# Moving where tiles start in SBUF: split inputs and DeltaNet outputs at multiples of 2048 bytes in a hybrid attention layer

## The chip, the cores and the metric

The kernel runs on one core of a Trainium2 chip. The metric is device time in microseconds (us) of one execution, the median over several runs. TensorE (PE) multiplies matrices; its weights are loaded by a queue of their own (PEld). VectorE (DVE), ScalarE (ACT) and GpSimd (POOL) work on tiles in SBUF; SyncE (SP) issues the DMAs. SBUF has 128 partitions, and a tile takes the same range of bytes in each of them, so "where a tile starts" is one byte offset within a partition.

## The reference

One layer of a diffusion backbone on 512 latent tokens after 256 context tokens, width 1024. All arithmetic is float32.

```python
hx = modulate(rms_norm(x), sh1, sc1);  hc = modulate(rms_norm(ctx), csh1, csc1)
ak, av, qkv, db, da, aq, z, gate = split_cols(hx @ w_in)     # context: the first columns only
attn_x = latent_attention(q_x, [k_c, k_x], [v_c, v_x])       # 8 heads of 128, 2 kv heads
o_x    = gdn_bidirectional(gdn_c_in, gdn_x_in)               # gated DeltaNet, 8 heads, both directions
gdn_x  = rms_norm(o_x, norm_w) * silu(z)
y = sigmoid(g_a) * (attn_x @ w_pa) + sigmoid(g_d) * (gdn_x @ w_pd)
x = x + g1 * (y @ w_out)
x = x + g2 * conv_ffn(modulate(rms_norm(x), sh2, sc2), w_up, ffn_conv_w, ffn_conv_b, w_down)
return rms_norm(x, final_norm_w)
```

Within a chunk the DeltaNet solves a unit lower triangular system `(I + strict(beta * dec * k k^T))`; everything else in it is small matrix products.

## The kernel before, in words

Every large product is made of three matmuls. A float32 operand is split in two words of a shorter format, `hi` (ACT copies and rounds) and `lo` (DVE subtracts), and `mm3` adds `hi*xh`, `hi*xl` and `lo*xh` in PSUM. The weights `whi`/`wlo` are the stationary operand, 128 columns at a time; the activations are the moving operand, 512 latent or 256 context columns at a time, 8 steps over the width. So one step of a latent projection is three 128x512 matmuls that read 2048 bytes of each partition of `xH` or `xL`.

The split activations are `hxH`/`hxL` (the modulated input, latent) and `hcH`/`hcL` (context), `atH`/`atL` (attention output), the `g` tiles (DeltaNet output), `yH`/`yL`, `h2H`/`h2L` and `aH`/`aL`. `at`, `y`, `h2` and `a` are allocated with `align_bytes=2048`. `hx` lies in the pool `hxp`, the first one on the right end of SBUF; it is read by 48 latent projections (24 of queries, keys and values, 8 of `z`, 16 of gates) and, as the stationary operand, by the attention's query, key and value projections (`pq`), and with the narrow weights `dbh`/`dbl` (32 columns) by the decays. The `g` tiles have no room of their own: `gsplit` puts them into slots of DeltaNet tiles that are no longer needed, `q4` (names `g_s`), `NN` (`g_n`), `kT` (`g_k`) and `M2` (`g_m`).

Pools are stacks: `cp` (constants and small columns), `ws` (weights) and then the pools of each stage grow from the left end, `hxp`, `stp`, `hcp` and later `yp`, `fp` from the right end. A pool that opens later lies over the bytes of one that was closed, and with `reuse_waits="tile"` a tile there waits for the old tiles that it overlaps.

The order is written out by hand: TensorE's instructions keep the program's order (`pinned`). During attention (about 190 to 362 us) the projections are woven between heads. After it come four pairs of DeltaNet heads. For a pair, `gdn_prep` loads `kT` and the decay rows `NN`, `Gb`; `gdn_solve` inverts the 32x32 diagonal blocks in 31 steps of two operations (`prod`, `R`), on POOL for pairs 1 to 3 and on DVE for pair 0, with `X`, `R`, `C`, `o_tr`, `o_nt` in three slots of the tag `q4`; `gdn_inv` completes the inverse on TensorE; `gdn_scan` runs over the chunks. The solve of the next pair runs beside the inverse and the scan of this one, and `weave` puts filling work (`filler`: the remaining projections, then `w_pa`, then `w_pd`) between them at fixed rates. From about 880 us on `w_out`, `w_up` and `w_down` follow with nothing woven in.

```python
q4 = lambda nm: gq.tile([P, 32, 32], F32, name=nm, tag="q4", bufs=3)
...
for j in range(31):
    ...
    tt(pv, X[:, j, j + 1:32].unsqueeze(2).to_broadcast([P, m, n]),
       R[:, j:j + 1, 0:n].to_broadcast([P, m, n]), ALU.mult, eng)
    tt(R[:, j + 1:32, 0:n], R[:, j + 1:32, 0:n], pv, ALU.add, eng)
```

Of the kernel before, what the change touches and what calls it, by code (L numbers as in the profile page):

```python
# [6 lines left out]
F32 = mybir.dt.float32  # L7
F32R = mybir.dt.float32r
# [6 lines left out]
P = 128  # L15
# [4 lines left out]
NA = NL + NCX  # L20
# [4 lines left out]
NH = 8  # L25
# [47 lines left out]
C_ID, C_ONE, C_MS, C_MI, C_TRI = 0, 128, 256, 512, 768  # L73
# [5 lines left out]
def hybrid_layer_body(tc, x, ctxt, xT, consts, cols, rows, w_mod1, w_mod2, w_db, w_aq, w_cm, w_pa, w_pd, w_out,  # L79
# [21 lines left out]
    es = ExitStack()  # L101
# [5 lines left out]
    def tt(out, a, b, op, eng=None):  # L107
        (eng or V).tensor_tensor(out=out, in0=a, in1=b, op=op)  # L108
# [7 lines left out]
    def stt(out, a, s, b, op0, op1):  # L116
        V.scalar_tensor_tensor(out=out, in0=a, scalar=s, in1=b, op0=op0, op1=op1)  # L117

    def act(out, a, f=AF.Copy, **kw):
        A.activation(out, a, f, **kw)  # L120
# [10 lines left out]
    def mm(ps, a, b, start=True, stop=True):  # L131
        T.matmul(ps, a, b, start=start, stop=stop)

    with es:
        cp = es.enter_context(tc.tile_pool(name="cp", bufs=1))
# [9 lines left out]
        def sooner():  # L145
            return tc.high_priority(offset=3000000)

        def solver():
            return tc.high_priority(offset=SOLVE)
# [1 line left out]
        def early():  # L151
            return tc.high_priority(offset=1000000)

        cst = cp.tile([P, C_TRI], F32, name="cst")
        with sooner():
            SP.dma_start(cst[:, 0:C_MS], consts[:, 0:C_MS])
        ident = cst[:, C_ID:C_ID + 128]
# [7 lines left out]
            ts(col[:, S_BMOD + o:S_BMOD + o + 8], col[:, S_BMOD + o:S_BMOD + o + 8], 1.0, ALU.add)  # L165
        mhalf = cp.tile([P, 32], F32, name="mhalf")
        V.memset(mhalf, -0.5)
        mod = cp.tile([P, 48], F32, name="mod")
        modc = cp.tile([P, 16], F32, name="modc")
        csl = cp.tile([P, KT], F32, name="csl")  # L170

# [43 lines left out]
        szd = [dp.tile([P, NL], F32, name=f"szd{i}") for i in range(NH)]  # L215
        atd = [dp.tile([P, NL], F32, name=f"atd{i}") for i in range(NH)]

        beta = cp.tile([P, 96], F32, name="beta")
        gam = cp.tile([P, 96], F32, name="gam")
        ngam = cp.tile([P, 96], F32, name="ngam")  # L220
        eg = cp.tile([P, 96], F32, name="eg")
        kdec = cp.tile([P, 96], F32, name="kdec")
        hks = [cp.tile([P, 6], F32, name=f"hk{i}") for i in range(NH)]
        glast = cp.tile([P, 96], F32, name="glast")
        qsc = [cp.tile([P, 8], F32, name=f"qsc{i}") for i in range(4)]
        rkk = [cp.tile([P, 6], F32, name=f"rkk{i}") for i in range(NH)]
# [188 lines left out]
        with m1_es:  # L415
# [11 lines left out]
            for op in LORD.split():  # L427
                i = int(op[1])
                with sooner():
# [3 lines left out]
                    elif op[0] == "h":  # L433
                        h, part = order[i]
# [421 lines left out]
        gq = ge.enter_context(tc.tile_pool(name="gq", bufs=1, reuse_waits="tile"))  # L856
# [15 lines left out]
        rqh = lambda p, hh: rkq[2 * p + hh]  # L872

        def gdn_prep(p, eng=G):
            kT = gq.tile([P, 2, NA], F32, name="kT", tag="kT", bufs=2)
            for hh in range(2):
                SP.dma_start(kT[:, hh, :], kTd[2 * p + hh])
            g = gq.tile([P, 32], F32, name="g", tag="g", bufs=2)
            gT = gq.tile([P, 32], F32, name="gT", tag="gT", bufs=2)
            V.memset(g[:, 24:32], 0.0)  # L880
            for d in range(2):
                for hh in range(2):
                    r0 = d * 48 + (2 * p + hh) * 6
                    u = slice(12 * d + 6 * hh, 12 * d + 6 * hh + 6)
                    stt(g[:, u], beta[:, r0:r0 + 6], -1.0, rkk[2 * p + hh], ALU.mult, ALU.mult)
                    tt(g[:, u], g[:, u], rkk[2 * p + hh], ALU.mult)
            V.transpose(gT, g)
            NN = gq.tile([P, 12, P], F32, name="NN", tag="NN", bufs=2)
            for hh in range(2):
                u = slice(6 * hh, 6 * hh + 6)  # L890
                Gb = gq.tile([P, 6, P], F32, name="Gb", tag="Gb", bufs=1)
                for d, D in ((0, NN[:, u, :]), (1, Gb)):
                    r0 = d * 48 + p * 12 + hh * 6
                    SP.dma_start(D.rearrange("p a b -> p (a b)"),
                                 gamdr[r0:r0 + 6, :].rearrange("a b -> (a b)").partition_broadcast(P))
                    tt(D, D, msk_s[d].unsqueeze(1).to_broadcast([P, 6, P]), ALU.add, eng)
                    for c in range(6):
                        act(D[:, c, :], D[:, c, :], AF.Exp, scale=-1.0, bias=gam[:, r0 + c:r0 + c + 1])
                tt(NN[:, u, :], NN[:, u, :], Gb, ALU.add, eng)
            return [kT, gT, NN]  # L900

        def gdn_solve(pre, eng):
            kT, gT, NN = pre
            for hh in range(2):
                for (c0, n) in ((0, 4), (4, 2)):
                    pb = gks.tile([P, 4, P], F32, name="pk", tag="pk")
                    for i in range(n):
                        sl = slice((c0 + i) * P, (c0 + i + 1) * P)
                        mm(pb[:, i, :], kT[:, hh, sl], kT[:, hh, sl])
                    u = slice(hh * 6 + c0, hh * 6 + c0 + n)  # L910
                    with sooner():
                        tt(NN[:, u, :], NN[:, u, :], pb[:, 0:n, :], ALU.mult)
                    yield
            with solver():
                q4 = lambda nm: gq.tile([P, 32, 32], F32, name=nm, tag="q4", bufs=3)
                C = q4("C")
                for b in range(4):
                    sb = slice(32 * b, 32 * b + 32)
                    V.transpose(C[sb, :, 12:24].rearrange("p j u -> p u j"), NN[sb, :, sb])
                    act(C[sb, :, 0:12], NN[sb, :, sb].rearrange("p u j -> p j u"))  # L920
                G.memset(C[:, :, 24:32], 0.0)
                X = q4("X")
                V.transpose(flat(X), flat(C))
                tt(X, X, gT.unsqueeze(2).to_broadcast([P, 32, 32]), ALU.mult)
                R = q4("R")
                G.memset(R, 0.0)
                G.memset(flat(R)[:, 0:1024:33], 1.0)
                if True:
                    for j in range(31):
                        m, n = 31 - j, j + 1  # L930
                        prod = gq.tile([P, 272], F32, name="prod", tag="prod")
                        pv = prod[:, 0:m * n].rearrange("p (i k) -> p i k", k=n)
# [3 lines that stand above are left out]
                tt(R, R, gT.unsqueeze(2).to_broadcast([P, 32, 32]), ALU.mult)  # L936
                o_tr = q4("o_tr")
                V.transpose(o_tr.rearrange("p u s -> p s u"), R)
                o_nt = q4("o_nt")
                V.transpose(o_nt.rearrange("p u s -> p s u"), R.rearrange("p i k -> p k i"))  # L940
            pre += [o_tr, o_nt]
# [210 lines left out]
        def gsplit(h):  # L1152
            if h % 2 == 0:
                if h < 4:
                    ts_ = [gq.tile([P, 32, 32], F32R, name="g_s", tag="q4", bufs=3) for _ in range(2 if h == 0 else 1)]
                    if h == 2:
                        ts_.append(gq.tile([P, 12, P], F32R, name="g_n", tag="NN", bufs=2))
                elif h == 4:
                    ts_ = [gq.tile([P, 12, P], F32R, name="g_n", tag="NN", bufs=2),
                           gq.tile([P, 2, NA], F32R, name="g_k", tag="kT", bufs=2)]  # L1160
                else:
                    ts_ = [gq.tile([P, 2, NA], F32R, name="g_k", tag="kT", bufs=2)]
                    ls = [gpool[0].tile([P, 2, 2, P], F32R, name="g_m", tag="M2", bufs=4) for _ in range(2)]
                    ls = [l.rearrange("p a b c -> p (a b c)") for l in ls]
                ts_ = [flat(t) for t in ts_]
                for i in range(2):
                    lo = ts_[1][:, 512 * i:512 * i + 512] if h < 6 else ls[i]
                    gHL[h + i] = (ts_[0][:, 512 * i:512 * i + 512], lo)
            return gHL[h]
# [13 lines left out]
        with early():  # L1183
            pre = gdn_prep(0, V if P0 else G)
# [113 lines left out]
        pinned[0] = True  # L1298
        weave(wait(WK), 1.0)
        weave(gdn_solve(pre, G if 0 in SPOOL else V), RK)  # L1300
        weave(wait(W0), 1.0)
        def stage(p, pre, nxt):
# [6 lines left out]
        for p in range(NP):  # L1309
            cur = pre  # L1310
            pre = gdn_prep(p + 1) if p + 1 < NP else None
            g = stage(p, cur, pre)
            weave(g, RI if p else RI0)
            while not gpool or len(ready) < 2 * p + 2:
                next(fill)
            g = gdn_scan(p, cur, gdn_load(p))
            out = (None, gdn_out(0), gdn_out(1), gdn_reload())[p]
            weave(both(g, out) if p > 0 else g, RS)
            weave(wait(W1), 1.0)
# [264 lines left out]
```

## Time and profile before

| | |
|---|---|
| median of 3 runs | 1305.97 us (1303.61 to 1308.03) |
| the profiled execution | 1306.96 us |
| its span, first to last instruction | 1304.3 us |
| mean granted TensorE clock | 0.978 |
| busy: PE, PEld, DVE, ACT, POOL | 94%, 79%, 65%, 48%, 24% |

The span is what the trace covers; 2.7 us of the execution lie around it. Matmuls are pipelined: the duration in a row runs until the result is out, and the next matmul starts before that, so the spacing of two starts tells the rate and the duration doesn't. The chain that ended last is followed back from the last instruction, at each step to what released it.

### The profile page before, as it was taken

The numbers are of one execution on the slowest core, as the hardware profiler recorded it, in microseconds if no ns is written. First come the engines' busy times: TensorE is split into PE (matmuls) and PEld (weight loads), VectorE is DVE, ScalarE is ACT, GpSimd is POOL, SyncE is SP. The second block draws the span as 40 slices with busy tenths as digits, with TensorE's granted clock in tenths as the row PEclk, the third lists the DMA queues.
The fourth block names the chain that finished last, engine by engine and source line by source line (L and its number), as shares of the span: only waits on it lengthen the run. The fifth ranks groups of instructions, "written<-read, shape, count | busy, mean of one in ns | idle before, by whom it ended". The sixth has DMA issues, their size and how long they took to land.

```text
span 1304.3 us, 20850 instructions
## 1 busy us (share of the span) xinstructions
PE 1229.6 (94%) x7835; PEld 1031.3 (79%) x7835; DVE 848.4 (65%) x1625; ACT 626.3 (48%) x1403; POOL 308.3 (24%) x364
## 2 busy tenths in 40 slices
PE   7899999999968999899998999999999999999997
PEld 4487878999857877778787878788988888888886
DVE  5886987777759986685665556555576666663323
ACT  5453656666576665474453443233354444443221
POOL 1752420000143249559447300000000000000000
PEclk8999999999998999899999999999999999999998
DMA  8656631121373342543533555265043222233331
GB/s 321 227 169 197 223 118 62 65 86 50 111 252 105 124 140 91 177 131 110 178 120 116 170 165 168 92 219 190 9 129 97 97 97 95 91 94 97 90 100 65
DMA packets 70789, 170.80 MB, mean 131 GB/s; under 512 B 7872, under 2 KB 18720, under 8 KB 69280
## 3 DMA queue, kind: packets, MB, share of 16 engines
q1 hardware_dynamic: 70688, 169.47, 39.4%
q8 instruction: 61, 1.00, 0.3%
q14 instruction: 40, 0.33, 0.1%
HBM read 144.23 MB, written 25.21 MB: 130 GB/s over the span
## 4 chain that ended last, share of the span: by engine, by line
PE 66%; POOL 10%; DVE 9%; DMA 5%; ACT 4%; issue 3%; SPq 0%; POOLq 0%; DVEq 0%; ACTq 0%
PE mc L87 32%; PE mb L87 17%; PE pq L87 4%; POOL R L108 4%; POOL prod L108 4%; PE pb L87 3%; PE pS L87 3%; PE ab L87 2%; PE ab L91 1%; DMA Gb<-gamdr 1%; PE xb L91 1%; DVE wlo L108 1%; PE pk L87 1%; DMA sz<-gdr 1%; POOL NN L108 1%
## 5 line engine op out<-in xcount | busy, mean ns | idle before, releaser
L108 DVE TENSOR_TENSOR wlo<-wraw,whi 128x1024 fp32r<-128x1024 f32 x152 | 187.6, 1235 | 162.6 <-ACT whi L120 161.6
L120 ACT ACTIVATE whi<-wraw 128x1024 fp32r<-128x1024 f32 x152 | 159.1, 1048 | 205.5 <-PE mc L87 106.5
L87 PE MATMUL mb<-hxH,whi 128*128 128x512 f32 x384 | 165.1, 430 | 2.1 <-DVE R L108 1.9
L87 PE MATMUL mb<-hxL,whi 128*128 128x512 f32 x384 | 155.0, 404 | 0.0
L87 PE MATMUL mb<-hxH,wlo 128*128 128x512 f32 x384 | 154.3, 402 | 0.0
L87 PE MATMUL mc<-h2L,whi 128*128 128x512 f32 (+1 forms) x376 | 142.7, 379 | 0.0
L87 PE MATMUL mc<-h2H,whi 128*128 128x512 f32 (+1 forms) x376 | 142.3, 378 | 0.3 <-ACT whi L120 0.3
L87 PE MATMUL mc<-h2H,wlo 128*128 128x512 f32 (+1 forms) x376 | 140.8, 374 | 0.5 <-DVE wlo L108 0.5
L108 POOL TENSOR_TENSOR rc<-rc,mhalf 128x2 f32<-128x2 f32 x4 | 3.3, 818 | 459.4 <-DVE rc L114 459.4
L87 PEld LDWEIGHTS mb<-hxH,wlo 128*128 128x128 f32 x384 | 74.0, 193 | 18.3
L87 PEld LDWEIGHTS mb<-hxH,whi 128*128 128x128 f32 x384 | 74.6, 194 | 13.9 <-ACT t L120 2.1
L87 PEld LDWEIGHTS mb<-hxL,whi 128*128 128x128 f32 x384 | 74.6, 194 | 10.3
L87 PEld LDWEIGHTS mc<-h2H,whi 128*128 128x128 f32 x376 | 70.6, 188 | 14.9 <-ACT whi L120 0.5
L87 PEld LDWEIGHTS mc<-h2H,wlo 128*128 128x128 f32 x376 | 70.6, 188 | 14.7 <-DVE wlo L108 1.0
L87 PEld LDWEIGHTS mc<-h2L,whi 128*128 128x128 f32 x376 | 70.7, 188 | 12.2
L87 PE MATMUL mc<-aH,whi 128*128 128x512 f32 (+1 forms) x198 | 72.9, 368 | 0.6 <-DVE x L117 0.6
L87 PE MATMUL mc<-aL,whi 128*128 128x512 f32 (+1 forms) x198 | 73.0, 369 | 0.0
L87 PE MATMUL mc<-aH,wlo 128*128 128x512 f32 (+1 forms) x198 | 72.0, 364 | 0.0
L117 DVE SCALAR_TENSOR_TENSOR u<-mc,col,u 128x511 f32<-128x511 f32 x88 | 65.3, 746 | 1.4
L108 POOL TENSOR_TENSOR prod<-X,R 128x31 f32<-128x31 f32 (+15 forms) x93 | 53.5, 576 | 22.3 <-DVE X L108 15.4
L108 POOL TENSOR_TENSOR R<-R,prod 128x31 f32<-128x31 f32 (+15 forms) x93 | 57.1, 613 | 6.8
L87 PE MATMUL pq<-whi,hxH 128*128 128x256 f32 x192 | 56.6, 295 | 0.0
(354 smaller groups left out, 3078.3 us busy)
## 6 DMA issues: line engine op xcount, KB each, us to landing
wraw<-in_w_cm_dram SPq DMA_DIRECT2D x48, 512.0 KB, 3.9
wraw<-in_w_up_dram SPq DMA_DIRECT2D x44, 512.0 KB, 3.7
wmd<-in_w_mod_dram SPq DMA_DIRECT2D x64, 256.0 KB, 3.8
wm<-in_w_mod_dram SPq DMA_DIRECT2D x8, 1024.0 KB, 8.2
wraw<-in_w_down_dram SPq DMA_DIRECT2D x16, 512.0 KB, 3.5
wraw<-in_w_aq_dram SPq DMA_DIRECT2D x12, 512.0 KB, 4.8
M<-gamdr SPq DMA_DIRECT2D x64, 64.0 KB, 4.4
wraw<-in_w_pa_dram SPq DMA_DIRECT2D x8, 512.0 KB, 4.0
```

Of the source, the lines that this page charges most:

```text
L87: i = nc.tensor.matmul(*a, **k)
L91: i = nc.tensor.transpose(*a, **k)
L108: (eng or V).tensor_tensor(out=out, in0=a, in1=b, op=op)
L117: V.scalar_tensor_tensor(out=out, in0=a, scalar=s, in1=b, op0=op0, op1=op1)
L120: A.activation(out, a, f, **kw)
```

## The change

A new pool `cr` on the right end, opened ahead of `hxp` and never closed, takes `cst`, `mod`, `beta`, `gam` and the first of the eight `hk` columns out of `cp`. The tags `kT`, `NN` and `q4`, and the `g` tiles that share their slots, are allocated with `align_bytes=2048`. No operation is added or removed.

```diff
+        cr = es.enter_context(tc.tile_pool(name="cr", bufs=1, side="right"))
-        cst = cp.tile([P, C_TRI], F32, name="cst")
+        cst = cr.tile([P, C_TRI], F32, name="cst")
...
-        mod = cp.tile([P, 48], F32, name="mod")
+        mod = cr.tile([P, 48], F32, name="mod")
...
-        beta = cp.tile([P, 96], F32, name="beta")
-        gam = cp.tile([P, 96], F32, name="gam")
+        beta = cr.tile([P, 96], F32, name="beta")
+        gam = cr.tile([P, 96], F32, name="gam")
...
-        hks = [cp.tile([P, 6], F32, name=f"hk{i}") for i in range(NH)]
+        hks = [(cp if i else cr).tile([P, 6], F32, name=f"hk{i}") for i in range(NH)]
...
-            kT = gq.tile([P, 2, NA], F32, name="kT", tag="kT", bufs=2)
+            kT = gq.tile([P, 2, NA], F32, name="kT", align_bytes=2048, tag="kT", bufs=2)
...
-            NN = gq.tile([P, 12, P], F32, name="NN", tag="NN", bufs=2)
+            NN = gq.tile([P, 12, P], F32, name="NN", align_bytes=2048, tag="NN", bufs=2)
...
-                q4 = lambda nm: gq.tile([P, 32, 32], F32, name=nm, tag="q4", bufs=3)
+                q4 = lambda nm: gq.tile([P, 32, 32], F32, name=nm, align_bytes=2048, tag="q4", bufs=3)
...
-                    ts_ = [gq.tile([P, 32, 32], F32R, name="g_s", tag="q4", bufs=3) for _ in range(2 if h == 0 else 1)]
+                    ts_ = [gq.tile([P, 32, 32], F32R, name="g_s", align_bytes=2048, tag="q4", bufs=3) for _ in range(2 if h == 0 else 1)]
```

The other tiles of `gsplit` (`g_n` twice, `g_k` twice) get the same argument; `g_m` does not.

## Rows read from the trace of the kernel before

**Rows 1.** The page: TensorE's busy time, share and instructions; the chain by engine.

```profile
PE 1229.6 (94%) x7835; PEld 1031.3 (79%) x7835; DVE 848.4 (65%) x1625; ACT 626.3 (48%) x1403; POOL 308.3 (24%) x364
...
PE 66%; POOL 10%; DVE 9%; DMA 5%; ACT 4%; issue 3%; SPq 0%; POOLq 0%; DVEq 0%; ACTq 0%
```

**Rows 2.** The chain in order of time, end of a solve: start us, us, what.

```profile
531.01 0.26 POOL R L108
...
533.18 1.83 DVE o_tr L938
...
537.08 2.08 PE pb L87 x8
```

**Rows 3.** TensorE in order of time: first and last matmul of five unbroken sequences.

```profile
100.31 0.39 PE L87 MATMUL mb<-hxH,dbh 128*32 128x512 f32 x1
...
105.59 0.39 PE L87 MATMUL mb<-hxH,dbl 128*32 128x512 f32 x1
...
748.34 0.40 PE L87 MATMUL mb<-hxL,whi 128*128 128x512 f32 x1
...
752.77 0.40 PE L87 MATMUL mb<-hxH,wlo 128*128 128x512 f32 x1
...
809.57 0.39 PE L87 MATMUL mb<-atL,whi 128*128 128x512 f32 x1
...
811.18 0.40 PE L87 MATMUL mb<-atH,wlo 128*128 128x512 f32 x1
...
848.01 0.40 PE L87 MATMUL mb<-g_s,wlo 128*128 128x512 f32 x1
...
853.60 0.39 PE L87 MATMUL mb<-g_s,wlo 128*128 128x512 f32 x1
...
1099.76 0.39 PE L87 MATMUL mc<-h2H,whi 128*128 128x512 f32 x1
...
1105.25 0.39 PE L87 MATMUL mc<-h2H,whi 128*128 128x512 f32 x1
```

**Rows 4.** Busy time by stretch, TensorE's instructions that read `hxL` alone.

```profile
190.00:365.00 175.00, 27.67 (x70) 1.00 0.23 80
365.00:420.00 55.00, 13.66 (x31) 0.88 0.52 170
420.00:468.00 48.00, 16.97 (x43) 1.00 0.38 125
468.00:537.00 69.00, 20.16 (x51) 0.99 0.40 130
537.00:566.00 29.00, 9.00 (x21) 0.90 0.44 137
566.00:631.00 65.00, 20.57 (x52) 1.00 0.40 127
631.00:664.00 33.00, 9.88 (x25) 0.95 0.52 167
664.00:718.00 54.00, 17.80 (x45) 0.99 0.35 117
718.00:760.00 42.00, 11.37 (x27) 0.93 0.58 180
```

**Rows 5.** The chain in order of time, the stretch of `w_pd`.

```profile
842.63 36.56 PE mb L87 x149
```

**Rows 6.** Groups of instructions by shape, DVE: two splits of 512 columns.

```profile
L108 DVE TENSOR_TENSOR aL<-u,aH 128x512 fp32r<-128x512 f32 x22 | 15.2, 691 | 14.0 <-ACT aH L120 14.0
...
L108 DVE TENSOR_TENSOR g_s<-sz,g_s 128x512 fp32r<-128x512 f32 x2 | 1.4, 692 | 2.6 <-ACT g_s L120 2.6
```

**Rows 7.** Tiles `QL` and `Gb`: durations, first and last start.

```profile
L87 PEld LDWEIGHTS pS<-KH,QL x64: 187/188/192, 186.3 to 343.2; 128*128 128x128 f32 x64
...
L894 SPq DMA_DIRECT2D Gb<-gamdr x8: 319/374/432, 357.1 to 578.3; - x8
```

**Rows 8.** TensorE's waits in 526:538 and 632:720; all engines in 538:546.

```profile
PE pb L87 <- DVE r L117: 4.2, 1, 4.2
...
PE pb L87 <- DVE r L117: 5.8, 2, 3.3
PE pb L87 <- DVE oacc L117: 2.7, 1, 2.7
...
538.00:546.00 8.00, 8.00 (x35) 6.78 (x35) 4.50 (x10) 2.96 (x9) 7.10 (x11) 0.71 0.42 137
```

More of the change, by code (lines that the diff above doesn't have):

```diff
@@ L1154, in gsplit @@
                 if h < 4:
-                    ts_ = [gq.tile([P, 32, 32], F32R, name="g_s", tag="q4", bufs=3) for _ in range(2 if h == 0 else 1)]
+                    ts_ = [gq.tile([P, 32, 32], F32R, name="g_s", align_bytes=2048, tag="q4", bufs=3) for _ in range(2 if h == 0 else 1)]
                     if h == 2:
-                        ts_.append(gq.tile([P, 12, P], F32R, name="g_n", tag="NN", bufs=2))
+                        ts_.append(gq.tile([P, 12, P], F32R, name="g_n", align_bytes=2048, tag="NN", bufs=2))
                 elif h == 4:
-                    ts_ = [gq.tile([P, 12, P], F32R, name="g_n", tag="NN", bufs=2),
-                           gq.tile([P, 2, NA], F32R, name="g_k", tag="kT", bufs=2)]
+                    ts_ = [gq.tile([P, 12, P], F32R, name="g_n", align_bytes=2048, tag="NN", bufs=2),
+                           gq.tile([P, 2, NA], F32R, name="g_k", align_bytes=2048, tag="kT", bufs=2)]
                 else:
-                    ts_ = [gq.tile([P, 2, NA], F32R, name="g_k", tag="kT", bufs=2)]
+                    ts_ = [gq.tile([P, 2, NA], F32R, name="g_k", align_bytes=2048, tag="kT", bufs=2)]
                     ls = [gpool[0].tile([P, 2, 2, P], F32R, name="g_m", tag="M2", bufs=4) for _ in range(2)]
```

## The prediction

> **What bounds the kernel now.** I read the page first, then the chain that ended last, then busy time by stretch, then single instructions in order of time. TensorE is busy for 94% of the span and carries 66% of the chain; POOL carries 10%, DVE 9%, DMA 5% [rows 1]. So the kernel is TensorE's, with holes. The holes are the DeltaNet solves: 31 pairs of small POOL operations in a row, at whose end DVE transposes the result (`o_tr`) and TensorE, which has run out of filling work, waits [rows 2]. In the order of time the chain is TensorE's from 190 to 365, 420 to 468, 537 to 566, 631 to 664 and from 718 us on; in 365 to 420, 468 to 537, 566 to 631 and 664 to 718 us it lies on DVE, DMA and POOL. The reader should see in this: a faster matmul in the first set of stretches moves the end, in the second it lengthens a wait.
>
> **What the change touches.** It changes where tiles begin, and hardly any instruction. In the kernel before, the right-hand stack of pools ends 32 bytes short of a multiple of 2048 (at byte 229344 of a partition; 112 x 2048 is 229376). `hxp` takes 32768 bytes, 16 x 2048, so `hxH`, every `hxL` and each of their 2048-byte rows (512 columns x 4 bytes) start 32 bytes below a multiple. The new pool `cr` holds 3072 (`cst`) + 192 (`mod`) + 384 + 384 (`beta`, `gam`) + 32 (`hk0`, padded) = 4064 bytes, and 4064 + 32 = 2 x 2048: below it `hxH` and `hxL` start on a multiple, at 225280 - 32768. All pools on the left lose the same 4064 bytes, so the free room between the two ends is what it was. `kT`, `NN` and `q4` begin 1504, 2016 and 992 bytes past a multiple now; with the argument they begin on one, and so do the `g_k`, `g_n`, `g_s` tiles in the same slots. `g_m` lies in `M2`, which gets no argument; it moves with its pool.
>
> **What a start is worth on TensorE.** I compare starts of successive matmuls of one shape (128x512, the same two-word split, each at the upper clock of 2.4 GHz, since 512 columns at 1.2 GHz alone would be 427 ns), because the durations in the rows overlap. Tiles that start off a multiple: `hx`, 19 steps from 748.34 to 752.77, 4.43/19 = 233.2 ns; the `g` tiles, 24 steps from 848.01 to 853.60, 5.59/24 = 232.9 ns. Tiles already on one: `h2`, 24 steps from 1099.76 to 1105.25, 5.49/24 = 228.8 ns; `at`, woven between DeltaNet work as `hx` mostly is, 7 steps from 809.57 to 811.18, 1.61/7 = 230.0 ns [rows 3]. So a start on a multiple goes with 2.9 to 4.4 ns less per matmul. One pair of rows speaks against reading this as a cause: the same `hxH` and `hxL`, off a multiple, against the 32-column weights `dbh` take 23 steps in 5.28 us, 229.6 ns [rows 3]. Either the cost of a bad start shows only beside a full 128-column weight load, or it isn't the start.
>
> A rule speaks for the second reading. The Trainium skill, SBUF — State Buffer, Who interferes with whom, gives TensorE two read ports of its own, one for the moving operand and one for the weights, and says that it never waits on anyone; nothing in it makes the place of a tile matter. By that rule the sum below is 0 and not 2.4 us. The rows of this case disagree to the extent that four spacings fall into two sets, though no single tile has been seen in both places.
>
> **The sum.** `hx` runs 8 steps of 3 matmuls of 512 columns in 48 projections, 1152 in all. The `hxL` matmuls, one in three, lie by stretch as follows: 70 + 43 + 21 + 25 + 27 = 186 in the stretches where TensorE is the chain, 31 + 51 + 52 + 45 = 179 in the others [rows 4]. (16 more are early, ahead of 92 us, where TensorE waits for the modulated input.)
> - `hx` on the chain: 186 x 3 = 558 matmuls. Per matmul I take 233.2 - 230.0 = 3.2 ns, by `at`, the tile that is woven the same way: 1.8 us. Bounds: 0, and 4.4 ns by `h2`, 2.5 us.
> - `g` tiles: `w_pd` reads 8 x 8 x 3 = 192 of them; 149 are in one unbroken piece of the chain from 842.63 us [rows 5]. 149 x (232.9 - 228.8) = 0.6 us; the `g_m` rows in it, one in twelve, I don't take off. The earlier 43 stand in a stretch whose chain is loads of `sz`, so 0.
> - `hx` off the chain: 179 x 3 = 537 matmuls, and 48 early ones. At 3.2 ns they free 1.9 us of TensorE, which I cost at 0: the POOL solve covers it, and what is late next is the wait at its end, which grows by the same time. If that cover were gone it would be a gain of up to 585 x 4.4 = 2.6 us.
> - Splits that write these tiles (ACT, DVE): 0. DVE takes 691 ns for `aL` (on a multiple) and 692 for `g_s` (off) [rows 6]. POOL on `X` and `R`, also moved: no row shows POOL on both kinds of start. By these DVE rows' 1 ns in 691, POOL's 10% of the chain [rows 1], 130 us, would move by 0.2 us either way; I take 0.
> - Matmuls of 256 columns (`hc`, the query and key projections, where `hx` is the weights): their moving tiles stay off a multiple, 0.
> - Waits for room: alignment adds at most 2016 bytes of slack to each of three tags, so tiles behind `kT` in `gq` and `gp` begin up to 6048 bytes further along and overlap other dead tiles of the attention. The added ones (`QL0` under `NN`, `QL2` under `Gb`) are last read at 343.2 us, and the first load into `Gb` is issued at 357.1 [rows 7]: 14 us of cover, so 0. Without it the load would queue on SP behind its wait, and the first solve with it. No DMA is added or moved.
>
> Sum: 1.8 + 0.6 = 2.4 us off. The profiled execution took 1306.96 us (span 1304.3 and 2.7 around it), which gives 1304.6. It lies 1.0 above the median of 1305.97, so against that median I predict 1303.6 us. About 0.3%, 3.9 us, is what a measurement of this kernel can tell from no change; the forecast is inside it.
>
> **The rivals.**
> *All of it lands.* The covered matmuls count too, since TensorE is busy for most of those stretches and its waits there are short (4.2 us is the longest after 420 us [rows 8]); a little reordering around the solves would hand the time on. Then 1152 x 4.4 + 192 x 4.1 = 5.1 + 0.8 = 5.9 us: 1300.1. Against it: TensorE works in a fixed order, and the solve's start follows TensorE while its end does not.
> *The start is not the cause.* The `dbh` rows at 229.6 ns are for it; the two sets of spacings are against it. Then nothing changes: 1306.0. The rule of the Trainium skill named above (SBUF — State Buffer, Who interferes with whom) would give this time too.
> *The clock takes it back, and more.* At the ends of the solves TensorE waits 4.2 us, then 5.8 us in two pieces and 2.7, and after the first of these the granted clock is 0.71 over 538 to 546 us [rows 8]: part of it is at 1.2 GHz, the rest at 2.4. The covered gain makes each of three such waits 0.5 to 0.7 us longer. If each then keeps the clock low for about as long again as it does here (0.29 x 8 = 2.3 us lost), it costs 6.9 us against 2.4 gained: 1310.5, slower. It decides once the three waits together lose more than 2.4 us beyond what they lose now, 0.8 us each. For it: the low clock stands right behind the waits. Against it: a tenth or so more of a wait that already brings the fall need not lengthen the fall.
>
> **Chances.** Forecast (only what lies on the chain) 0.48, all lands 0.28, start not the cause 0.14, clock 0.10. Faster by over 0.3% is the second case and a few hundredths of the first, where 4.4 ns holds and the rest partly lands: 0.31. Slower by over 0.3% is the worse half of the clock case: 0.06. Within: 0.63. The range goes from all landing, 1300.0, over the forecast (its own range, by its bounds, 1302.9 to 1306.0) and no change to a mild clock loss, 1307.5, about 1.5 above the median; below and above that I leave out some 0.15.
>
> **What would show it.** `hx` and `g_k`/`g_n`/`g_s` steps at 229 to 230 ns instead of 233; if they stay at 233, the start is not the cause. The woven attention, 190 to 365 us, should shorten by about 210 x 3.2 = 0.7 us and the `w_pd` stretch from 842 us by 0.6. The waits before `o_tr` should grow by half a microsecond each, and the POOL pairs keep their times. The prediction is wrong if the solve stretches themselves get shorter, if DVE or POOL operations on `X`, `R` or `NN` change by more than a few ns, or if the granted clock after the solves falls for longer.

## The result and the profile after

The changed kernel takes 1308.97 us, median of 22 runs (1305.49 to 1313.34), against 1305.03 us of the kernel before in the same job, also 22 runs (1301.88 to 1308.03): a ratio of 1.0036, 95% interval 1.0026 to 1.0045, so 3.4 to 5.9 us slower. The prediction said 1303.6 us, with 1307.5 as its upper end and 0.06 for slower.

The profiled execution of the changed kernel took 1307.51 us with a span of 1305.7, only 0.55 us more than that of before. The granted clock differs between these two executions (mean 0.987 against 0.978), so in what follows the profiles tell where time goes, and the runs tell how much. The two lines of the page that answer to [rows 1], busy time by engine and the chain by engine:

```profile
PE 1228.8 (94%) x7835; PEld 1024.2 (78%) x7835; DVE 847.5 (65%) x1625; ACT 625.4 (48%) x1403; POOL 309.0 (24%) x364
...
PE 64%; POOL 10%; DVE 10%; DMA 5%; issue 4%; ACT 3%; SPq 0%; DVEq 0%; POOLq 0%; ACTq 0%
```

They show nothing: the same engine bounds the kernel with the same busy share. What changed stands in the view behind [rows 3], TensorE's instructions of the changed kernel in order of time; first and last of four unbroken sequences:

```profile
364.07 0.39 PE L87 MATMUL mb<-hxH,whi 128*128 128x512 f32 x1
...
368.50 0.40 PE L87 MATMUL mb<-hxL,whi 128*128 128x512 f32 x1
...
754.37 0.40 PE L87 MATMUL mb<-atH,whi 128*128 128x512 f32 x1
...
756.00 0.39 PE L87 MATMUL mb<-atL,whi 128*128 128x512 f32 x1
...
841.44 0.39 PE L87 MATMUL mb<-g_s,whi 128*128 128x512 f32 x1
...
846.79 0.39 PE L87 MATMUL mb<-g_s,wlo 128*128 128x512 f32 x1
...
939.39 0.39 PE L87 MATMUL mc<-h2H,whi 128*128 128x512 f32 x1
...
943.82 0.40 PE L87 MATMUL mc<-h2L,whi 128*128 128x512 f32 x1
```

`hx`: 19 steps in 4.43 us, 233.2 ns, as before, although it now starts on a multiple of 2048. The `g` tiles: 23 steps in 5.35 us, 232.6 ns, as before, although they too start on one now. And `h2`, which started on a multiple of 2048 in both kernels: 19 steps in 4.43 us, 233.2 ns, where it was 228.8 [rows 3]. `at`, on a multiple in both: 7 steps in 1.63 us, 232.9 ns against 230.0. So the tiles that moved gained nothing, and tiles that kept their start modulo 2048 lost 3 to 4 ns a matmul. The undisturbed end (`mc`: `w_out`, `w_up`, `w_down`) in order of time, its first matmul and its last group, of the kernel before:

```profile
879.03 0.40 PE L87 MATMUL mc<-yH,whi 128*128 128x512 f32 x1
...
1296.97 0.84 PE L87 MATMUL mc<-dg,cst 128*128 128x128 f32 x3
```

and of the changed kernel:

```profile
872.86 0.40 PE L87 MATMUL mc<-yH,whi 128*128 128x512 f32 x1
...
1297.26 0.68 PE L87 MATMUL mc<-dg,cst 128*128 128x128 f32 x4 [1.50 <-DVE dg L112]
```

Up to the start of the last matmul in that group (1297.39 before, 1297.66 after) it takes 418.4 us before and 424.8 after.

Something else went the other way, in a stretch that the prediction left alone: TensorE's longest wait ahead of the first solve. TensorE's waits and all engines by stretch (the figure behind POOL's is the granted clock) in 365 to 420 us, of the kernel before:

```profile
PE pk L87 <- DVE NN L108: 8.8, 1, 8.8
...
365.00:420.00 55.00, 40.59 (x210) 33.79 (x210) 44.24 (x71) 39.55 (x113) 25.53 (x19) 0.88 0.52 170
```

and of the changed kernel:

```profile
PE pk L87 <- DVE NN L108: 0.6, 1, 0.6
...
365.00:420.00 55.00, 46.36 (x253) 39.28 (x252) 50.41 (x90) 39.40 (x112) 20.13 (x12) 0.94 0.40 131
```

The wait is down to 0.6 us, and the granted clock of the stretch rose from 0.88 to 0.94, since less of it is at 1.2 GHz. The cause is on SP. Before, `vtok`, `ktok` and the 16 loads of `M` for the first scan were issued among the loads of `Gb` for the solve. SP's DMAs of the kernel before in order of time, then pieces of its chain, then the instruction of DVE that they release (in brackets its idle time and the releaser):

```profile
361.02 0.52 SPq L1006 DMA_DIRECT2D vtok<-vtd  x1
...
367.14 6.33 SPq L1023 DMA_DIRECT2D M<-gamdr  x7
...
376.37 0.38 SPq L894 DMA_DIRECT2D Gb<-gamdr  x1
```

```profile
376.79 7.33 DMA M<-gamdr
384.18 0.73 POOL M L108
385.25 0.39 ACT M L120
385.83 1.55 ACT Gb L120 x5
```

```profile
387.42 0.96 DVE L108 TENSOR_TENSOR NN<-NN,Gb 128x768 f32<-128x768 f32 x1 [4.67 <-ACT Gb L120]
```

ACT's exponential of `M` stands in its queue ahead of that of `Gb`; it waits for POOL and the last `M` load, and the second product into `NN`, the matrix that the solve needs, waits 4.67 us for it, until 387.42. In the changed kernel the `Gb` loads come first, and those of the scan only from 418.6 us on; SP, and the same product on DVE:

```profile
372.14 9.26 SPq L895 DMA_DIRECT2D Gb<-gamdr  x2
```

```profile
380.10 0.95 DVE L108 TENSOR_TENSOR NN<-NN,Gb 128x768 f32<-128x768 f32 x1
```

That is 7.3 us earlier on DVE, of which the runs below that turn the order in the kernel before leave 2.6 to 4.0 us at the end. In the twelve kernels with the layer, order and wait go together: TensorE's longest wait before `pk` is 6.1 to 9.9 us in the six with the old order and 0.6 in the six with the new one. TensorE's waits at the ends of the later solves [rows 8] stayed as they were, 4.2 us the longest.

### The profile page after: what moved, and what is told of

It is laid out like the page before. It is cut to its first block, busy times and chain, and to the rows that moved or that the text cites. A ratio compares the mean times of both kernels' runs of the same rounds, so it can differ in the third digit from the quotient of the medians.

```text
span 1305.7 us, 20854 instructions
## 1 busy us (share of the span) xinstructions
PE 1228.8 (94%) x7835; PEld 1024.2 (78%) x7835; DVE 847.5 (65%) x1625; ACT 625.4 (48%) x1403; POOL 309.0 (24%) x364
## 4 chain that ended last, share of the span: by engine, by line
PE 64%; POOL 10%; DVE 10%; DMA 5%; issue 4%; ACT 3%; SPq 0%; DVEq 0%; POOLq 0%; ACTq 0%
PE mc L87 32%; PE mb L87 16%; POOL R L108 4%; POOL prod L108 4%; PE pq L87 3%; PE pb L87 3%; PE pS L87 3%; PE ab L87 2%; DMA Gb<-gamdr 2%; PE ab L91 1%; DVE wlo L108 1%; PE xb L91 1%; DMA sz<-gdr 1%; PE pk L87 1%; DVE R L108 1%
```

## The experiments

Where tiles lie, as bytes modulo 2048; the changed kernel's pool took 4064 bytes from the left end, and 4064 is 63.5 x 64, so the weights moved too:

| kernel | weights | `hx` | `g` slots (`kT`, `NN`, `q4`) | `h2`, `a`, `y`, `at` |
|---|---|---|---|---|
| before | 1984 | 2016 | 1504, 2016, 992 | 0 |
| changed | 2016 | 0 | 0 | 0 |

Four readings of this were open when the first four runs went in. M, that of the prediction: the start of the moving tile counts alone. W: the start of the weights counts alone. P: it is the pair, in its first form whether both have the same remainder by 64. O: the first solve's order is worth its time independent of starts on TensorE.

**The weights moved**, by a dead tile of 32 bytes in the kernel before (weights 2016, `hx` 2016). The `g` slots move by 32 bytes with them; `hx`, `h2`, `a`, `y` and `at` keep their starts modulo 2048:

```diff
+        cp.tile([P, 8], F32, name="pad")
```

> The kernel before with one dead tile of 32 bytes at the end of the left-hand constants: every tile on the left moves by 32 bytes, so the weights whi/wlo go from a start at 0 to one at 32 past a multiple of 64; hx stays at 32, h2, a, y and at stay at 0. Theory W (a matmul of 512 columns is short only when both the weights and the moving tile start on a multiple of 64): h2, a, y, at rise from 229 to 233 ns, 1758 matmuls x 4.4 = 7.7 us slower, hx stays at 233; about 1313 us. Theory P (short when both have the same remainder by 64): h2, a, y, at rise likewise, but hx falls to 229 and gives back 2.5 to 5 us; about 1309. Theory M of the prediction (only the moving tile's place counts): all spacings stay, 1305.

Measured: 1309.39 us, ratio 1.0047 (1.0029 to 1.0065). TensorE in order of time, `hx` and `h2`:

```profile
364.22 0.39 PE L87 MATMUL mb<-hxH,whi 128*128 128x512 f32 x1
...
368.54 0.39 PE L87 MATMUL mb<-hxL,whi 128*128 128x512 f32 x1
...
941.23 0.39 PE L87 MATMUL mc<-h2H,whi 128*128 128x512 f32 x1
...
945.66 0.40 PE L87 MATMUL mc<-h2L,whi 128*128 128x512 f32 x1
```

`hx` did not move and fell to 4.32/19 = 227.4 ns; `h2` kept its start and rose to 4.43/19 = 233.2. One edit of 32 bytes to the weights changed both, in opposite directions. M falls on both, W on `hx`, which it had at 233; the pair is what counts.

**The change, with the weights back on a multiple** (the same dead tile in the changed kernel; weights, `hx`, `g`, `h2` all 0):

> The changed kernel with the same dead tile of 32 bytes: weights at a multiple of 2048 as well as hx, the g tiles and the rest. W and P: every 512-column spacing at 229 ns; against the changed kernel 7.7 us off for h2, a, y and at, 2.5 us for hx on the chain and 0.6 for g; about 1298 us. M: spacings stay as in the changed kernel, 233 ns, 1309.

Measured: 1294.98 us, ratio 0.9934 (0.9917 to 0.995), the fastest of all kernels with the layer, and 3 us under what W and P expected.

```profile
935.95 0.39 PE L87 MATMUL mc<-h2H,whi 128*128 128x512 f32 x1
...
940.25 0.39 PE L87 MATMUL mc<-h2L,whi 128*128 128x512 f32 x1
```

4.30/19 = 226.3 ns: `h2` is now shorter than in the kernel before, which the remainder by 64 (0 in both) does not explain.

**Only `hx` moved**, to 1984, the weights' own place, by 32 dead bytes on the right end:

> The kernel before with 32 dead bytes at the right end ahead of hx: hx starts at 1984 past a multiple of 2048, which is a multiple of 64, as the weights already do; the g tiles stay at 32. W and P: hx at 229 ns, 2.5 us (chain only) to 5 us off, 1300 to 1302.5. M with a step of 2048: hx stays at 233, 1305.

Measured: 1303.32 us, ratio 0.9995 (0.9983 to 1.0008): no difference that the runs can tell, so the time expected, 2.5 to 5 us off, was missed, although the spacing fell.

```profile
436.11 0.39 PE L87 MATMUL mb<-hxH,whi 128*128 128x512 f32 x1
...
440.41 0.39 PE L87 MATMUL mb<-hxL,whi 128*128 128x512 f32 x1
```

4.30/19 = 226.3 ns, and 229.8 as a mean over all its sequences (233.1 before): `hx` is short 64 bytes away from any multiple of 2048. The prediction's 1.8 us for this term lies inside the interval, as does zero.

**Only the slots aligned** (the kernel before with the argument on `kT`, `NN`, `q4` and the `g` tiles):

> The kernel before with the argument for kT, NN, q4 and the g tiles alone; constants, weights and hx stay. Theory O (the slots' places change which old tiles a new one waits for, and with that the planned order of loads after the attention): TensorE's wait of 8.8 us before pk near 381 us shrinks to about 1 as in the changed kernel, some 8 us off; with g at 229 ns 0.6 more; 1296 to 1298. If the first solve's gain comes from the moved constants or weights: g alone, 1304.

Measured: 1301.3 us, ratio 0.9974 (0.996 to 0.9989): 4.0 us between the medians and 3.4 by the ratio, half of what O expected. `g` fell to 229.9 ns on average; TensorE's wait before `pk` fell to that of the changed kernel:

```profile
PE pk L87 <- DVE NN L108: 0.6, 1, 0.6
```

**Only the slots moved along, none aligned**: the kernel before with a dead tile at the beginning of `gp`.

```diff
+            gpool[0].tile([P, 1512], F32, name="gpad")
```

> The kernel before with nothing aligned, only a dead tile of 6048 bytes at the beginning of the pool gp, so that the tiles of the solve lie as far along as the slots' alignment puts them. Theory O (the gain of the slots-only version is not from its starts but from where those tiles lie, over other tiles of the attention, which turns the order of SP's loads: Gb ahead of the next scan's loads) expects TensorE's wait before the first solve's pk to fall from 8.8 us to about 1 and a time of 1301 to 1302, with g still at 233 ns. If alignment itself brought that gain, this run is at 1305.

Measured: 1302.71 us, ratio 0.9977 (0.9965 to 0.9989), 2.6 us between the medians and 3.0 by the ratio; `g` at 232.7 ns, the same 0.6 us before `pk`. So O holds in its mechanism, and without any alignment: with the pool 6048 bytes further along the order of loads changes. Which older tile under `vtok`, `ktok` and `M` turns it was not tried.

**Only the pool** (the changed kernel without the argument; weights 2016, `hx` 0):

```diff
-            kT = gq.tile([P, 2, NA], F32, name="kT", align_bytes=2048, tag="kT", bufs=2)
+            kT = gq.tile([P, 2, NA], F32, name="kT", tag="kT", bufs=2)
...
```

> The changed kernel without the argument on kT, NN, q4 and the g tiles: the new pool alone. Theory P (what counts is the start of the moving tile against the start of the weights, modulo 64; the pool moved the weights by 4064 bytes, 32 past a multiple of 64) expects h2, a, y and at at 233.3 ns as in the changed kernel, hx 233 and g 233; the first solve keeps its old order and its wait of nearly 9 us before pk. So slower than the changed kernel by the 4 us of that order: about 1313, ratio to before 1.006 (+7.7 us). The theory that the slots' argument is what costs the time in the changed kernel expects this run at or below the kernel before, 1303 to 1305.

Measured: 1310.79 us, ratio 1.0047 (1.0033 to 1.0062), 6 us more than before and nearer to 1313 than to 1304. `h2`, `a`, `y` 233.3 ns, and the old order with its wait:

```profile
PE pk L87 <- DVE NN L108: 6.5, 1, 6.5
```

The pool costs the time in the changed kernel. What the slots give back in it is 1.4 us by the two ratios (1.0047 here, 1.0036 changed); their intervals overlap, so the trace shows the shorter wait, and these two runs alone don't show its gain.

**Weights 64 bytes past a multiple**, everything else on one:

```diff
+        cp.tile([P, 24], F32, name="pad")
```

> The version with everything on a multiple, but the weights 64 bytes past a multiple of 2048 instead of on one (as in the kernel before, where they were 64 short of one). If the remainder by 64 is all, h2, a and y keep 226.7 ns and the time stays at 1295. If the last 2 ns of that version come from weights on a multiple of 2048 (or 128), h2, a and y return to 228.9 and g to 229 and the time is 2 to 3 us longer, about 1298.

Measured: 1311.49 us, ratio 1.0037 (1.0017 to 1.0056). `h2`, `a`, `y` took 233.3 ns. Both forecasts missed: 64 past a multiple costs the full price, where 64 short of one (the kernel before) costs 228.9. The remainder by 64 is not the rule.

**High words on, low words 32 bytes off** (a dead tile between `whi` and `wlo`, in the kernel with everything on):

```diff
+            if pool is None:
+                ws.tile([P, 8], F32, name="wpad", tag="wpad", bufs=1)
```

> The version with everything on a multiple, with a dead 32-byte tile between the two weight buffers, so the high words wh start on a multiple of 64 and the low words wl 32 bytes past one. A block of 512 columns is three passes: high by high, high by low, low by high. If the stream clashes with the weights that it uses itself, only the low-by-high pass becomes longer, by 13 to 20 ns (three times the mean difference of 4.4 to 6.6, as a mean over the three is what was seen so far); if it clashes with the load of the weights that come next, which runs beside it, it is the pass ahead of a load of wl. If the cost has nothing to do with the weights' start, all three keep 226.7 on average.

Measured: 1312.39 us in a single run. Three passes in order of time:

```profile
1000.42 0.40 PE L87 MATMUL mc<-h2L,whi 128*128 128x512 f32 x1
1000.66 0.39 PE L87 MATMUL mc<-h2H,wlo 128*128 128x512 f32 x1
1000.89 0.40 PE L87 MATMUL mc<-h2H,whi 128*128 128x512 f32 x1
1001.12 0.40 PE L87 MATMUL mc<-h2L,whi 128*128 128x512 f32 x1
```

The long step is 1000.42 to 1000.66: the pass `h2L,whi`, both operands on a multiple. Over all 328 it is 239 ns (the middle value), where `h2H,wlo`, whose own weights are off, takes 228 and `h2H,whi` 233. So a pass is not slowed by the start of the weights that it uses itself. The long pass is the one beside which `wlo` is loaded, which speaks for a clash with the load of the next weights; but `h2H,whi` also runs 6 ns over, which this reading does not explain.

**The disputed cost by itself.** Nothing of the layer is computed: after a load and a split, TensorE alone runs the three passes over 8 steps, with starts set by slicing four tiles (high and low words of both operands) that begin on a multiple of 2048. 28 cases, four banks each, in one order and then in reverse.

```diff
+                for k in range(8):
+                    w = lambda t, o: t[:, o // 4 + k * P:o // 4 + k * P + P]
+                    x_ = lambda t: t[:, xo // 4 + k * NL:xo // 4 + k * NL + NL]
+                    mm3(ps, w(wH, wo), w(wL, wl), x_(xH), x_(xL), k, 8)
```

> The disputed cost by itself: nothing of the layer is computed, only sequences of the same two-word matmul (three passes of 128x512 a step, eight steps a bank, four banks a case, each case twice) with the start of the weights (W) and of the moving rows (M), modulo 2048, set by hand; all other engines idle. The runs so far: W 0, M 0 226.7 ns a matmul; W 1984, M 0 228.9; W 2016, M 0 233.3; W 64, M 0 233.3; W 1984, M 2016 233.1; high words 0, low words 32, M 0 233.3. The theory of the remainder by 64 has fallen on W 64. Theory D (what counts is the distance W minus M): W 64, M 64 and W 2016, M 2016 cost as W 0, M 0, 226.7; W 1984, M 2016 costs as W 2016, M 0, 233.3; W 0, M 64 as W 1984, M 0, 228.9. Theory A (each operand's own place counts, the weights' above all): W 64 costs 233 whatever M is, and W 0 costs 227 to 229 whatever M is. In both, W 512 and 1024 with M 0 tell whether a weight block's place counts by 512 (a block is 512 bytes long): then both cost as W 0. Third, if the spacings of the kernel come from what the other engines do meanwhile and not from the starts, all cases here are equal.

First and last matmul of five cases, 95 steps each, in order of time (weights, moving rows: 0, 0; 64, 0; 256, 0; 0, 32; 64, 64):

```profile
43.60 0.39 PE L91 MATMUL w_x<-xH,wH 128*128 128x512 f32 x1
...
65.14 0.40 PE L91 MATMUL w_x<-xH,wL 128*128 128x512 f32 x1
...
87.76 0.40 PE L91 MATMUL w_x<-xH,wH 128*128 128x512 f32 x1
...
109.93 0.39 PE L91 MATMUL w_x<-xH,wL 128*128 128x512 f32 x1
...
176.91 0.39 PE L91 MATMUL w_x<-xH,wH 128*128 128x512 f32 x1
...
198.44 0.40 PE L91 MATMUL w_x<-xH,wL 128*128 128x512 f32 x1
...
353.71 0.40 PE L91 MATMUL w_x<-xH,wH 128*128 128x512 f32 x1
...
375.88 0.40 PE L91 MATMUL w_x<-xH,wL 128*128 128x512 f32 x1
...
530.50 0.39 PE L91 MATMUL w_x<-xH,wH 128*128 128x512 f32 x1
...
552.05 0.39 PE L91 MATMUL w_x<-xH,wL 128*128 128x512 f32 x1
```

21.54 us, 22.17, 21.53, 22.17 and 21.55: 226.7, 233.4, 226.6, 233.4 and 226.8 ns. All the cases with one start for both words, by the distance of the weights' start from that of the moving rows, modulo 256 (worked out from the starts in the trace):

| distance | cases (weights, moving) | ns a matmul |
|---|---|---|
| 0 | 0,0; 256,0; 512,0; 1024,0; 0,512; 0,1024; 32,32; 64,64; 512,512; 2016,2016 | 226.7 to 227.1 |
| 32 or -32 | 32,0; 480,0; 2016,0; 0,32; 0,2016; 1984,2016 | 233.2 to 233.4 |
| 64 | 64,0; 0,1984 | 233.3 to 233.4 |
| -64 | 192,0; 448,0; 1984,0; 0,64 | 228.9 to 229.0, or 233.3 |
| 96 | 96,0 | 234.2 |
| 128 | 128,0; 384,0; 0,128 | 232.3 to 233.3 |

The distance decides (theory D), and what repeats is 256 bytes. At -64 there are two spacings: 448,0 took 233.3 ns in the first order and 228.9 in the reverse one, 1984,0 the other way round. All other engines were idle and the granted clock was 0.999, so no neighbour makes this cost.

Two of the 28 cases have a start for each word. With the low words alone at 32 a matmul takes 233.4 and 233.2 ns in the two orders, and the three passes 232, 239 and 228, as in the kernel. With the high words alone at 32 it takes 231.8 in both, and the passes 232, 231 and 233. Three passes of the second case and the loads beside them, in order of time:

```profile
642.05 0.39 PE L91 MATMUL w_x<-xH,wH 128*128 128x512 f32 x1
642.06 0.19 PEld L91 LDWEIGHTS w_x<-xL,wH 128*128 128x128 f32 x1
642.29 0.39 PE L91 MATMUL w_x<-xL,wH 128*128 128x512 f32 x1
642.29 0.19 PEld L91 LDWEIGHTS w_x<-xH,wL 128*128 128x128 f32 x1
642.51 0.39 PE L91 MATMUL w_x<-xH,wL 128*128 128x512 f32 x1
```

Each load starts with the pass before its own. If only the load of the next weights counted, the pass `xL,wH`, beside which the low words at 0 are loaded, would take 227 ns here and not 231. So that the distance sets the cost is shown; which transfer holds up which, and why 256 bytes, is not.

**The rule back in the kernel, 1**: the kernel before, weights moved by 64 dead bytes to 0.

```diff
+        cp.tile([P, 16], F32, name="pad")
```

> The kernel before with one dead 64-byte tile at the end of the pool cp and nothing else: the weights move from 1984 to 0 modulo 2048, so their distance to h2, a, y and at becomes 0; hx stays at 2016, a distance of 32. By the rule that the sequences by themselves gave (shortest where the distance is a multiple of 256 bytes) h2, a and y fall from 228.9 to 226.7 ns and hx and g stay at 233. h2, a and y have 522 steps of three matmuls: 1566 x 2.2 = 3.4 us; the order of loads and the first wait before pk stay as they were. So about 1302, ratio 0.9973. If the rule does not carry over to the kernel, h2 keeps 228.9 or goes to 233 and the time is 1305 or more.

Measured: 1303.37 us, ratio 0.9977 (0.9964 to 0.999): 1.3 to 4.7 us off. `h2` and `a` at 226.7 ns, `y` 226.9, `hx` 232.6, `g` 233.1.

**The rule back in the kernel, 2**: all on, but the slots on multiples of 256.

```diff
-            kT = gq.tile([P, 2, NA], F32, name="kT", align_bytes=2048, tag="kT", bufs=2)
+            kT = gq.tile([P, 2, NA], F32, name="kT", align_bytes=256, tag="kT", bufs=2)
...
```

> The version with everything on a multiple, but the argument of kT, NN, q4 and the g tiles 256 instead of 2048, so these tiles begin at 1792, 256 and 1536 modulo 2048 and the pools behind them lie 5376 bytes lower. By the rule of 256 every spacing stays as it was with 2048: h2, a, y 226.7, g 227.3, hx 229.5. The tiles no longer move 6048 bytes along, the order of SP's loads is that of the kernel before again, so theory O expects the wait of 7 to 9 us before the first pk to come back and the time to be 3 to 4 us longer than with 2048: about 1298.5, ratio 0.995. If the 4 us came from the alignment by 2048, not from the order, the spacing of g or of the solve's operations changes instead, and the wait stays under 1 us.

Measured: 1299.21 us, ratio 0.9961 (0.9942 to 0.9979). `h2`, `a`, `y` 226.7 ns, `g` 227.5, `hx` 229.3, and the wait is back:

```profile
PE pk L87 <- DVE NN L108: 9.2, 1, 9.2
```

So every spacing stays with 256, and what 2048 goes with beyond that is the order: 4.2 us between the medians of these two kernels (1299.21 and 1294.98), 3.5 us by their ratios, whose intervals meet at their ends.

## Why the prediction was wrong

**The time of the end by the distance.** From the first to the last `mc` matmul TensorE sets the pace; it waits 3.8 us in all, in the kernel before as in the changed one. In the twelve kernels with the layer this stretch falls into three sets:

| distance of weights and `h2`, `a`, `y` | kernels | ns a matmul | the stretch, us |
|---|---|---|---|
| 0 | weights on; all on; all on 256 | 226.7 | 415.2 to 415.7 |
| -64 | before; `hx` moved; slots only; shifted only | 228.9 | 418.4 to 418.7 |
| -32; 64; 0 and 32 by word | changed; weights off; pool only; weights 64; low words off | 233.3 | 424.3 to 425.3 |

It holds 328 + 154 + 40 = 522 steps of `h2`, `a` and `y`, 1566 matmuls; 1566 x 4.4 ns = 6.9 us between the last two sets, and the rows give 5.6 to 6.9.

**Point by point.**
- "What a start is worth on TensorE" failed. Its two sets of spacings were there, but it put them down to where the moving tile starts. Shown: it is the distance to the weights, whose place the part "What the change touches" passed over with "All pools on the left lose the same 4064 bytes, so the free room between the two ends is what it was". The room was; the place of the weights was not.
- The sum's first two terms, `hx` 1.8 and `g` 0.6 us, measured 0 in their spacings: `hx` and the weights went from 2016 and 1984 to 0 and 2016, distance -32 in both, and the `g` slots are at -32 modulo 256 in both kernels too. The spacing taken for `hx` was about right for a kernel in which the distance does go to 0 (229.8 ns in the run with `hx` moved, against the 230.0 taken), but by luck: the 230.0 is that of `at`, at a distance of -64.
- A term was missing: 1566 matmuls of `h2`, `a`, `y` and 192 of `at`, at distance -64 before and -32 after: 1566 x 4.4 + 192 x 3.2 ns = 7.5 us lost. The run with the pool alone, which has this term and not the new order, is 6.1 us slower by its ratio (4.3 to 8.1).
- "Waits for room: 0" failed with the other sign. It asked whether a load would wait longer for its slot, and costed 6048 bytes of shift at nothing; it did not ask whether SP's queue would be ordered anew. It was: in the kernel before, the shift without alignment is worth 2.6 us between the medians, the slots alone 4.0, of which `g` has 149 x 3.4 ns = 0.5. In the changed kernel `g` gains nothing, which leaves 2.6 to 3.5.
- Together 7.5 less 2.6 to 3.5 is 4.0 to 4.9 us slower; 3.9 lie between the medians, and the interval is 3.4 to 5.9. The same prices account for the fastest kernel: 3.2 us of the end, 558 x 3.5 ns = 2.0 of `hx`, 149 x 6.0 ns = 0.9 of `g` and 2.6 to 3.5 of the order are 8.7 to 9.6 us; by its ratio it is 8.6 faster (6.5 to 10.8).
- Right were: ACT, DVE and POOL at 0 (DVE's split `aL` takes 692 ns after, 691 before [rows 6]; POOL's `R` 613 ns on average in both), and that the clock costs nothing (the mean granted clock did not fall). The waits at the later solves did not grow by the half microsecond that "What would show it" asked for; `hx` got no faster.
- The rival "the start is not the cause" had the fact that spoke for it, `dbh` at 229.6 ns [rows 3], and its sign came true: `hx` and `g` stayed at 233. Its time, 1306.0, did not, because it too looked at one operand alone. With `dbh` at 192 and `hx` at 2016 the distance is -32 at the first step, not a multiple of 256, but only 32 columns of weights are loaded; that the shorter load makes it cheap was not tried.

The Trainium skill, SBUF — State Buffer, Who interferes with whom, says that TensorE's two read ports are independent and names only the pair of ports that VectorE and GpSimd share as a place of contention. The sequences by themselves differ from it: with every other engine idle, the spacing of 226.7 ns grows by up to 7.5 with the distance between the starts of moving rows and weights alone, by 6.6 at 32. The measurement decides here.

## What to carry to other kernels

Place weights and moving rows of a long run of matmuls at the same start modulo 256 bytes (shown here for 128x512 matmuls of this two-word split, each with its own weight load; other shapes and types were not tried); a round number for one of them alone says nothing, and whatever is taken from a pool in front of the weights moves them too. When tiles are moved, list the new start of every operand of the busiest engine, those that were not meant to move above all, and compare the order of the DMA queue in both kernels. Where spacings of one shape fall into two sets, an edit of 32 bytes to each operand in turn tells which of them, or which pair, makes the difference.

## What was not expected of the hardware

- The distance of -64 bytes has two spacings, 228.9 and 233.3 ns, both seen for the same starts within one execution (448,0: 22.16 us for 95 steps from 220.99, 21.75 from 1082.94); what chooses between them was not found. 64 on the other side had only 233.3 to 233.4.
- The first solve's wait goes with a lower clock: in the five kernels with the layer that have the old order beside the kernel before (weights off, `hx` moved, pool only, weights on, all on 256) the granted clock in 365 to 420 us is 0.88, as it is there; in the changed kernel, slots only and shifted only it is 0.94, with weights 64 and low words off 0.97, and 1.00 with everything on.
- A single profile of each kernel would have misled: the two profiled executions differ by 0.55 us and the medians by 3.9. Their granted clocks differ too (0.987 after, 0.978 before); that this makes up the rest is not shown.
